# A hybrid convolution and attention block: wider steps for taps and attention, softmax scaled on ScalarE, norm sums in other PSUM banks

## The chip, the cores and the metric

The kernel runs on one core of a Trainium2 chip. The metric is the device time of one execution in microseconds (us); the time before is the median of three runs. Engines: TensorE (PE) multiplies matrices, VectorE (DVE) and ScalarE (ACT) work elementwise on SBUF and PSUM, GpSimd (POOL) elementwise on SBUF, and SyncE's queue (SP) issues the transfers.

## What is computed

```python
h = rmsnorm(x, norm_g)                                   # x: 2048 x 1024, fp32
proj = h @ w_in                                          # 1024 x 7680
glu_in, conv_gate, q, k, v, attn_gate, merge_logits = split(proj)

a, b = split(glu_in)                                     # convolution branch
c = depthwise_conv(a * sigmoid(b), w_dw, 31 taps, causal) + b_dw
c = silu(layernorm(c, ln_g, ln_b))                       # over the 1024 channels
y_conv = (c * silu(conv_gate)) @ w_conv_out

q, k = rope(q), rope(k)                                  # 16 q heads, 4 kv heads, 64 wide
s = (q @ k.T) * 64 ** -0.5                               # 128-wide sliding window
m = max(rowmax(s), sink);  p = exp(s - m)
a = (p / (sum(p) + exp(sink - m))) @ v
y_attn = (a * silu(attn_gate)) @ w_attn_out

g_conv, g_attn = split(sigmoid(merge_logits))
x = x + (g_conv * y_conv + g_attn * y_attn) @ w_out
return rmsnorm(x, final_norm_g)
```

## The kernel before

The 2048 positions are worked in two sweeps of 1024. Activations stand transposed (channels on partitions) as pairs of fp32r tiles, a rounded part and its remainder, and so do weights; each product takes three matmuls (rounded by rounded, rounded by remainder, remainder by rounded). A projection of 128 output channels over a sweep is one *item* (`project`): two halves of 512 positions, 24 matmuls each into one of three PSUM banks (`mm_ps`), and then an evacuation of the half by ACT or DVE. An item's weights are loaded and split one item ahead (`load_w`: SP loads, ACT casts, POOL subtracts).

A sweep runs 12 items for k, v and q with RoPE (`rope_items`, L426: DVE multiplies out of PSUM, POOL adds, ACT and DVE split, SP stores to DRAM), then 32 gate items (`gate_item`, L404: ACT applies Silu or Sigmoid into a `t2k` tile, which is stored to DRAM), then eight items `ya` (attention output), eight `yc` (convolution output) and sixteen blocks `o` (output projection). In between, ahead of items 0, 4, 8 to 28 of these 44 (`GLU_AFTER`), stand eight pairs of GLU items, one for each 128 channels of the convolution.

Only PE's order is written by hand; the other engines' orders are the framework's scheduling of the same program. The hand order comes from a planner with a clock of its own, the class `Line` (L160). It counts 0.2275 us for a matmul (`MM_US`), and `spend` puts in, after each three matmuls, what is due:

- *Taps.* The 31 taps of a channel tile (`conv_ops`, L359; DVE, L368) go to a queue `bg` when the tile's GLU is done. One leaves it every `line.every` us, `CONV_EVERY` at first.
- *Attention.* `start_attention` (L588) sets 32 steps of one kv head and 128 positions each, the n-th at 8.0 + n * `ATT_EVERY`. A step (`attention`, L512) comes in three parts, `LAT[0]` and `LAT[1]` apart: eight score matmuls `sc` (L526), masking and softmax (L533 to L548); four transposes `tpp` (L553) with a split (L555, L230) and selects for the two key blocks (L562, L564); four products `ov` (L573) with the sum (L577) and a store (`d_att`, L578). A step loads q and k for the next one (`load_qk`, L495).
- *Layer norm.* When the eighth tile has its last tap, `ln_chain` (L636) splits the channel sum into four `t2k` tiles, and after `LN_LAT[0]` sums over partitions by matmuls with ones (`ln_stats`, L606, in the bank of the scores, `sc_ps`); ACT copies the mean (L641). Eight `ln_center` follow, one every `LN_EVERY`; then `ln_chain2` does the same for the variance after `LN_LAT[1]`, with ACT's square root (L652), four reciprocals (`ln_recip`) and eight `ln_apply` (DVE product, ACT Silu, L634).
- *The attention output's inputs.* During the last gate item sixteen `aT` steps (`a_op`, L700) are put into the queue, 14 when the last attention is done, two when the norm is done. Before the first `ya` matmul, `line.finish()` empties the queue.

`slot` names one of 40 fixed SBUF places; `next_of` goes round in a ring of them. There are five `t2k` tiles for all uses.

Of the kernel before, what the change touches and what calls it, by code (L numbers as in the profile page):

```python
# [12 lines left out]
F32 = mybir.dt.float32  # L13
F32R = mybir.dt.float32r
I32 = mybir.dt.int32
AF = mybir.ActivationFunctionType
ALU = mybir.AluOpType
AX = mybir.AxisListType

P = 128  # L20
S = 2048
D = 1024
KC = D // P
T = 1024
NSWEEP = S // T
NB = T // P
TH = 512
# [5 lines left out]
GQ = NH // NKV  # L33
# [5 lines left out]
EPS = 1e-5  # L39
NEG = -1e30  # L40
MM_US = 0.2275
LN_LAT = (9.0, 15.0)
LN_EVERY = 2.4
GLU_AFTER = (0, 4, 8, 12, 16, 20, 24, 28)
CONV_EVERY = 2.0
ATT_EVERY = 13.4
LAT = (16.0, 12.0)
SCALE = HD ** -0.5


# [1 line left out]
def hybrid_block(ctx: ExitStack, tc: tile.TileContext, x, par_d, w_in, w_conv, sinks, w_attn, w_out,  # L52
                 fin_g, rope_t, out):
    nc = tc.nc
    pe, act, dve, pool = nc.tensor, nc.scalar, nc.vector, nc.gpsimd
# [4 lines left out]
    work = ctx.enter_context(tc.tile_pool(name="work", bufs=2))  # L60
    mm_ps = ctx.enter_context(tc.tile_pool(name="mm_ps", bufs=3, space=bass.MemoryType.PSUM))
    tp_ps = ctx.enter_context(tc.tile_pool(name="tp_ps", bufs=3, space=bass.MemoryType.PSUM))
    sc_ps = ctx.enter_context(tc.tile_pool(name="sc_ps", bufs=1, space=bass.MemoryType.PSUM))
# [5 lines left out]
    def f(ap):  # L69
        return ap.bitcast(F32)  # L70
# [7 lines left out]
    def slot(tag, shape, dt, name):  # L78
        n = int(np.prod(shape[1:]))
        full = HALO + T + 2 if tag in WIDE else 1024  # L80
        t = slots.tile([P, full], dt, tag=tag, name=name)
        v = t[:, 0:n]
        if len(shape) == 3:
            v = v.rearrange("p (a b) -> p a b", b=shape[2])
        elif len(shape) == 4:
            v = v.rearrange("p (a b c) -> p a b c", b=shape[2], c=shape[3])
        return v
# [6 lines left out]
    def next_of(key, tags):  # L94
        rot.setdefault(key, cycle(range(len(tags))))
        return tags[next(rot[key])]
# [20 lines left out]
    ones = const.tile([P, P], F32R, name="ones")  # L117
# [9 lines left out]
    eps = eps[:, 0:1]  # L127
# [219 lines left out]
    def sweep(s):  # L347
# [147 lines left out]
        def load_qk(n):  # L495
            if n >= NKV * NB:
                return
            g, b = divmod(n, NB)
            blk = s * NB + b
            t = slot(next_of("qk", AT[11:14]), [P, 2, 4 * P], F32R, f"qk{s}_{n}")  # L500
            q, k = t[:, 0, :].rearrange("p (r t) -> p r t", t=P), t[:, 1, :].rearrange("p (a t) -> p a t", a=2)
            qk[n] = (q, k)
            fs = slice(g * HH, (g + 1) * HH)
            for i in range(4):
                nc.sync.dma_start(out=f(q[i * HH:(i + 1) * HH]), in_=d_q[i // 2, i % 2, fs, blk, :, :])
            k0 = max(blk - 1, 0) * P
            nk = (blk + 1) * P - k0
            for i in range(4):
                nc.sync.dma_start(out=f(k[i * HH:(i + 1) * HH, :, 2 * P - nk:]),
                                  in_=d_k[:, i % 2, fs, k0:k0 + nk].rearrange("a p t -> p a t"))  # L510

        def attention(n):  # L512
# [7 lines left out]
            for h in range(GQ):  # L520
                for j in range(2):
# [2 lines left out]
                    else:  # L524
                        o, r = sc[:, h], k[:, j]
                    pe.matmul(out=o, lhsT=q[:, h, :], rhs=r, start=(j == 0), stop=(j == 1))  # L526
            ss = slot(next_of("ss", AT[4:7]), [P, 1024], F32, f"ss{u}")
            sb = ss[:, 0:512].rearrange("p (h q) -> p h q", q=P)
            oT = ss[:, 512:768].rearrange("p (a q) -> p a q", q=P)
            if first:  # L530
# [1 line left out]
            else:  # L532
                act.copy(sb, sc[:, :, 0, :])  # L533
            dve.copy_predicated(out=sb, mask=causal_i, data=sc[:, :, 1, :])
            st = work.tile([P, 6, GQ], F32, tag="st", name=f"st{u}", bufs=3)
            mx, ngm, es, den, rinv, dlt = (st[:, i, :] for i in range(6))
            hd = slice(g * GQ, (g + 1) * GQ)
            dve.tensor_reduce(out=mx, in_=sb, axis=AX.X, op=ALU.max, negate=True)
# [6 lines left out]
                               bias=ngm[:, h:h + 1], accum_out=den[:, h:h + 1])  # L545
            dve.tensor_tensor(out=den, in0=den, in1=es, op=ALU.add)
            dve.reciprocal(out=rinv, in_=den)  # L547
            pool.tensor_tensor(out=sb, in0=sb, in1=rinv.unsqueeze(2).broadcast_to([P, GQ, P]), op=ALU.mult)  # L548
            yield 0.96, LAT[0]

            tpp = tp_ps.tile([P, GQ, P], F32, tag="tp", name=f"tpp{u}")
# [5 lines left out]
            if first:  # L557
                seq = [(v_of(g, b), pt)]
            else:
                pc = slot(next_of("pc", AT[9:11]), [P, 2, GQ, P], F32R, f"pc{u}")  # L560
                for i in range(2):
                    pool.affine_select(out=pc[:, i], in_=f(pt[:, i]), pattern=[[0, GQ], [1, P]],  # L562
                                       compare_op=ALU.is_ge, fill=0.0, base=0, channel_multiplier=-1)
                    pool.affine_select(out=pt[:, i], in_=f(pt[:, i]), pattern=[[0, GQ], [-1, P]],  # L564
                                       compare_op=ALU.is_gt, fill=0.0, base=0, channel_multiplier=1)
                seq = [(v_of(g, b), pc), (v_of(g, b - 1), pt)]
            yield 0.44, LAT[1]

# [19 lines left out]
        def start_attention():  # L588
            load_qk(0)
            for n in range(NKV * NB):  # L590
                line.after(8.0 + n * ATT_EVERY, attention(n))


        ln = {}
# [10 lines left out]

        def ln_stats(parts, name):  # L606

            st = sc_ps.tile([P, T], F32, tag="sc", name=f"{name}{s}")
            for half in range(2):
                for i in range(2):  # L610
                    pe.matmul(out=st[:, half * TH:(half + 1) * TH], lhsT=ones, rhs=parts[half][i],
                              start=(i == 0), stop=(i == 1))
            return st

        def ln_center(c):
# [20 lines left out]
        def ln_chain():  # L636
            parts = ln_parts(csum, "csum")
            yield 0.0, LN_LAT[0]
            st = ln_stats(parts, "lnmu")
            ln["mu"] = slot(AT[15], [P, T], F32, f"mu{s}")  # L640
            act.copy(ln["mu"], st)  # L641
            line.every = LN_EVERY
            line.bg.extend([lambda c=c: ln_center(c) for c in range(KC)])
            line.bg.append(lambda: line.start(ln_chain2()))
            yield 4 * MM_US, 0.0

        def ln_chain2():
            parts = ln_parts(ln["v"], "vsum")
            yield 0.0, LN_LAT[1]
            st = ln_stats(parts, "lnvar")  # L650
            ln["r"] = slot(AT[14], [P, T], F32, f"rstd{s}")
            act.activation(out=ln["r"], in_=st, func=AF.Sqrt, bias=eps)  # L652
            work_ops = [lambda i=i: ln_recip(i) for i in range(4)]
            work_ops += [lambda c=c: ln_apply(c) for c in range(KC)]
            work_ops.append(lambda: ln.update(done=True))
            line.bg.extendleft(reversed(work_ops))
            yield 4 * MM_US, 0.0
# [3 lines left out]
        gates += [gate_item("ma", C_MA, AF.Sigmoid, e) for e in range(KC)]  # L661
        gates += [gate_item("mc", C_MC, AF.Sigmoid, e) for e in range(KC)]
        line.every = CONV_EVERY
        others = rope_items("k", E_K, store_k) + [v_item(i) for i in range(2)]
        for r in range(GQ):
            others += rope_items(f"q{r}_", E_Q + 2 * r, store_q(r))
# [4 lines left out]
        if s == 0:  # L671
# [8 lines left out]
                    yield ((lambda: None) if half == i == 0 else item[half][0],) + item[half][1:]  # L680
            glu_after.pop(0)
        for i, item in enumerate(others):
            if glu_after and i == glu_after[0]:
                glu_after.pop(0)
                items = glu_items(KC - 1 - len(glu_after))
                yield from items
            if s or i:
                yield item
            if i == nqkv:
                start_attention()  # L690


        aT, uT = [[None] * KC, [None] * KC], []
# [200 lines left out]
```

## Time and profile before

| | |
|---|---|
| median of 3 runs | 2235.6 us (2234.0 to 2236.23) |
| the profiled execution | 2237.25 us |
| its span, first to last instruction | 2235.5 us |
| busy: PE, DVE, POOL, ACT | 94%, 67%, 45%, 41% |
| PE's mean granted clock | 0.968 |
| first PE instruction; last | 8.5 us; 2229 us |

A page of the profile gives busy time by engine, the chain of waits that ended last, and groups of instructions by line: operation, output and inputs, count, busy time in us, mean ns of one, then the idle time of the engine just before them and what ended it. The view of waits has rows "engine, tile and line, waited for whom: us in total, times, longest". A timeline row has start (us), duration (us), engine, line, operation; in square brackets the idle time ahead of it and what ended that. A window row gives the window, its length, and each engine's busy time (with its count of instructions), then PE's granted clock, the share of the DMA engines, GB/s. The first row of matmuls of each stage gives the stage boundaries used below.

### The profile page before, as it was taken

The page shows a single profiled execution, that of the slowest core. Times are in us where ns is not written, and L with a number is a line of the kernel's source. Part 1 is how long each engine was busy: PE and PEld are TensorE (multiplying, and loading weights), DVE is VectorE, ACT ScalarE, POOL GpSimd, SP SyncE. Part 2 cuts the span into 40 slices and gives each one's busy share as a digit, 9 for nine tenths or more (in the row PEclk, how much of TensorE's full clock was granted, in tenths as well). Part 3 has the DMA queues.
Part 4 walks back from the last instruction along what each step waited for, and adds up shares of the span by engine and source line. Part 5 has one row for each costly group of instructions (what it writes and reads, how often), then busy time and mean ns, then how long its engine had stood idle before and what let it go on. Part 6 is the DMA issues. An engine that isn't in the chain of part 4 may idle for free. (4 is left out here: it accounts for less than half of the span.)

```text
span 2235.5 us, 26989 instructions
## 1 busy us (share of the span) xinstructions
PE 2105.8 (94%) x9256; PEld 1694.8 (76%) x9256; DVE 1505.9 (67%) x1804; ACT 918.0 (41%) x1925; POOL 995.9 (45%) x738
## 2 busy tenths in 40 slices
PE   7999899899999889999999999999899899899998
PEld 6877678778777766888887777777777777668887
DVE  4999988697797417123678999696797973261224
ACT  5212254555557723123522113545556486231212
POOL 4446556575655421241033545665656654112400
PEclk9999999999999997999999999999999999889999
DMA  5223433323333247334322324333333333572331
GB/s 182 80 90 108 134 98 96 106 93 114 102 110 110 90 146 240 104 100 168 114 95 90 108 90 123 111 105 108 101 97 104 100 106 104 172 222 92 99 127 76
DMA packets 186873, 257.81 MB, mean 115 GB/s; under 512 B 21616, under 2 KB 87280, under 8 KB 186736
## 3 DMA queue, kind: packets, MB, share of 16 engines
q1 hardware_dynamic: 186736, 256.09, 36.1%
q8 instruction: 73, 1.20, 0.2%
q14 instruction: 64, 0.52, 0.1%
HBM read 184.70 MB, written 71.30 MB: 115 GB/s over the span
## 5 line engine op out<-in xcount | busy, mean ns | idle before, releaser
L368 DVE SCALAR_TENSOR_TENSOR cv<-glu,par,cv 128x1024 f32<-128x1024 f32 x480 | 764.9, 1594 | 9.5
L259 PE MATMUL mm_ya<-aT,whi_ya 128*128 128x512 f32 x512 | 183.9, 435 | 22.6 <-ACT aT L271 18.7
L564 POOL TENSOR_SCALAR_AFFINE_SELECT pt<-pt 128x512 fp32r<-128x512 f32 x120 | 128.0, 1069 | 126.0 <-DVE st L541 53.4
L815 PE MATMUL o<-wo,mT 128*128 128x512 f32 x768 | 180.7, 394 | 0.0
L259 PE MATMUL mm_ga<-hT,whi_ga 128*128 128x512 f32 x512 | 163.7, 401 | 13.8 <-DVE rb_q__1_10475 L438 3.4
L815 PEld LDWEIGHTS o<-wo,mT 128*128 128x128 f32 x768 | 143.3, 188 | 31.4
L259 PE MATMUL mm_gb<-hT,whi_gb 128*128 128x512 f32 x512 | 166.1, 406 | 0.0
L259 PE MATMUL mm_cg<-hT,whi_cg 128*128 128x512 f32 x512 | 163.2, 400 | 0.0
L259 PE MATMUL mm_ag<-hT,whi_ag 128*128 128x512 f32 x512 | 162.1, 398 | 0.0
L259 PE MATMUL mm_ma<-hT,whi_ma 128*128 128x512 f32 x512 | 161.7, 397 | 0.0
L259 PE MATMUL mm_mc<-hT,whi_mc 128*128 128x512 f32 x512 | 161.5, 397 | 0.0
L562 POOL TENSOR_SCALAR_AFFINE_SELECT pc<-pt 128x512 fp32r<-128x512 f32 x120 | 123.3, 1030 | 84.6 <-ACT pt L555 76.2
L259 PE MATMUL mm_yc<-uT,whi_yc 128*128 128x512 f32 x512 | 159.4, 392 | 0.0
L259 PEld LDWEIGHTS mm_ya<-aT,whi_ya 128*128 128x128 f32 x512 | 103.1, 201 | 70.0 <-ACT aT L271 35.5
L548 POOL TENSOR_TENSOR ss<-ss,st 128x512 f32<-128x512 f32 x64 | 94.8, 1482 | 127.4 <-DVE st L547 34.9
L544 ACT ACTIVATE ss<-ss,st 128x128 f32<-128x128 f32 x256 | 99.8, 391 | 119.1 <-DVE st L539 118.8
L230 POOL TENSOR_TENSOR wlo_ya<-raw_ya,whi_ya 128x512 fp32r<-128x512 f32 x32 | 42.6, 1330 | 190.3 <-ACT whi_ya L240 190.3
L259 PEld LDWEIGHTS mm_ga<-hT,whi_ga 128*128 128x128 f32 x512 | 96.7, 192 | 36.6 <-issue 15.4
L259 PEld LDWEIGHTS mm_gb<-hT,whi_gb 128*128 128x128 f32 x512 | 98.8, 196 | 21.4
L259 PEld LDWEIGHTS mm_mc<-hT,whi_mc 128*128 128x128 f32 x512 | 97.3, 191 | 21.7
L259 PEld LDWEIGHTS mm_yc<-uT,whi_yc 128*128 128x128 f32 x512 | 96.1, 188 | 21.9
L259 PEld LDWEIGHTS mm_cg<-hT,whi_cg 128*128 128x128 f32 x512 | 96.6, 193 | 20.5
(357 smaller groups left out, 4741.2 us busy)
## 6 DMA issues: line engine op xcount, KB each, us to landing
qk<-d_q SPq DMA_DIRECT2D x256, 64.0 KB, 2.7
qk<-d_k SPq DMA_DIRECT2D x240, 64.0 KB, 2.3
raw_gb<-in_w_in_dram SPq DMA_DIRECT2D x34, 256.0 KB, 2.7
raw_ga<-in_w_in_dram SPq DMA_DIRECT2D x34, 256.0 KB, 3.1
raw_ag<-in_w_in_dram SPq DMA_DIRECT2D x32, 256.0 KB, 3.0
d_ag<-ag SPq DMA_DIRECT2D x32, 256.0 KB, 2.5
d_att<-ss SPq DMA_DIRECT2D x64, 128.0 KB, 1.8
raw_cg<-in_w_in_dram SPq DMA_DIRECT2D x32, 256.0 KB, 2.8
```

What stands on the lines that cost most here:

```text
L230: eng.tensor_tensor(out=out_, in0=full, in1=f(hi), op=ALU.subtract)
L259: pe.matmul(out=ps, lhsT=a, rhs=b, start=(k == 0 and i == 0), stop=(k == KC - 1 and i == 2))
L368: dve.scalar_tensor_tensor(out=cv[c], in0=glu[c][:, j:j + T], scalar=tap(c, j), in1=cv[c], op0=ALU.mult, op1=ALU.add)
L544: act.activation(out=sb[:, h, :], in_=sb[:, h, :], func=AF.Exp, scale=SCALE, bias=ngm[:, h:h + 1], accum_out=den[:, h:h + 1])
L548: pool.tensor_tensor(out=sb, in0=sb, in1=rinv.unsqueeze(2).broadcast_to([P, GQ, P]), op=ALU.mult)
L562: pool.affine_select(out=pc[:, i], in_=f(pt[:, i]), pattern=[[0, GQ], [1, P]], compare_op=ALU.is_ge, fill=0.0, base=0, channel_multiplier=-1)
L564: pool.affine_select(out=pt[:, i], in_=f(pt[:, i]), pattern=[[0, GQ], [-1, P]], compare_op=ALU.is_gt, fill=0.0, base=0, channel_multiplier=1)
L815: pe.matmul(out=ps, lhsT=a[:, c0:c0 + P], rhs=r, start=(k == 0 and i == 0), stop=(k == KC - 1 and i == 2))
```

## The change

Six edits, all in how the same work is placed:

1. Taps leave the queue every 2.4 us of the planner's clock instead of 2.0.
2. Attention steps are 14.5 apart instead of 13.4; the latencies inside a step are 22 and 14 instead of 16 and 12. The ring of softmax tiles `ss` has four places instead of three (it takes one from the ring `qk`, three to two), and the small statistics tile `st` has four buffers instead of three.
3. Attention is set up before the first item after the last q item (a GLU pair's first) instead of after that pair, and its first step is due 22 us from there instead of 8.
4. The division of the softmax is four ACT copies with a scale for each partition, one for each head, instead of one POOL product with a broadcast.
5. The four POOL selects become two, each over both parts of the split.
6. The norm's sums go to two tiles of the projections' banks (`mm_ps`) instead of the scores' bank, with the copy and the square root in two halves; the latencies before them are 14 and 30 instead of 9 and 15.

```diff
-LN_LAT = (9.0, 15.0)
+LN_LAT = (14.0, 30.0)
-CONV_EVERY = 2.0
-ATT_EVERY = 13.4
-LAT = (16.0, 12.0)
+CONV_EVERY = 2.4
+ATT_EVERY = 14.5
+LAT = (22.0, 14.0)
...
-            t = slot(next_of("qk", AT[11:14]), [P, 2, 4 * P], F32R, f"qk{s}_{n}")
+            t = slot(next_of("qk", AT[11:13]), [P, 2, 4 * P], F32R, f"qk{s}_{n}")
...
-            ss = slot(next_of("ss", AT[4:7]), [P, 1024], F32, f"ss{u}")
+            ss = slot(next_of("ss", AT[4:7] + AT[13:14]), [P, 1024], F32, f"ss{u}")
...
-            st = work.tile([P, 6, GQ], F32, tag="st", name=f"st{u}", bufs=3)
+            st = work.tile([P, 6, GQ], F32, tag="st", name=f"st{u}", bufs=4)
...
-            pool.tensor_tensor(out=sb, in0=sb, in1=rinv.unsqueeze(2).broadcast_to([P, GQ, P]), op=ALU.mult)
+            for h in range(GQ):
+                act.activation(out=sb[:, h, :], in_=sb[:, h, :], func=AF.Copy, scale=rinv[:, h:h + 1])
...
-                for i in range(2):
-                    pool.affine_select(out=pc[:, i], in_=f(pt[:, i]), pattern=[[0, GQ], [1, P]],
-                                       compare_op=ALU.is_ge, fill=0.0, base=0, channel_multiplier=-1)
-                    pool.affine_select(out=pt[:, i], in_=f(pt[:, i]), pattern=[[0, GQ], [-1, P]],
-                                       compare_op=ALU.is_gt, fill=0.0, base=0, channel_multiplier=1)
+                pool.affine_select(out=pc, in_=f(pt), pattern=[[0, 2], [0, GQ], [1, P]],
+                                   compare_op=ALU.is_ge, fill=0.0, base=0, channel_multiplier=-1)
+                pool.affine_select(out=pt, in_=f(pt), pattern=[[0, 2], [0, GQ], [-1, P]],
+                                   compare_op=ALU.is_gt, fill=0.0, base=0, channel_multiplier=1)
...
-                line.after(8.0 + n * ATT_EVERY, attention(n))
+                line.after(22.0 + n * ATT_EVERY, attention(n))
...
-            st = sc_ps.tile([P, T], F32, tag="sc", name=f"{name}{s}")
+            st = []
             for half in range(2):
+                st.append(mm_ps.tile([P, TH], F32, tag="mm", name=f"{name}{s}_{half}"))
                 for i in range(2):
-                    pe.matmul(out=st[:, half * TH:(half + 1) * TH], lhsT=ones, rhs=parts[half][i],
-                              start=(i == 0), stop=(i == 1))
+                    pe.matmul(out=st[half], lhsT=ones, rhs=parts[half][i], start=(i == 0), stop=(i == 1))
             return st
...
-            act.copy(ln["mu"], st)
+            for half in range(2):
+                act.copy(ln["mu"][:, half * TH:(half + 1) * TH], st[half])
...
-            act.activation(out=ln["r"], in_=st, func=AF.Sqrt, bias=eps)
+            for half in range(2):
+                act.activation(out=ln["r"][:, half * TH:(half + 1) * TH], in_=st[half], func=AF.Sqrt, bias=eps)
...
         for i, item in enumerate(others):
+            todo = [item] if s or i else []
             if glu_after and i == glu_after[0]:
                 glu_after.pop(0)
-                items = glu_items(KC - 1 - len(glu_after))
-                yield from items
-            if s or i:
-                yield item
+                todo = glu_items(KC - 1 - len(glu_after)) + todo
             if i == nqkv:
-                start_attention()
+                todo[0] = ahead(todo[0], start_attention)
+            yield from todo
```

`ahead(item, work)` is an item that does `work` when its first matmul is planned.

More of the change, by code (lines that the diff above doesn't have):

```diff
@@ L663, in sweep, with ahead, blocks @@
         line.every = CONV_EVERY
+        def ahead(item, work):
+            def blocks():
+                work()
+                yield from item[1]()
+            return item[0], blocks
         others = rope_items("k", E_K, store_k) + [v_item(i) for i in range(2)]
```

## The prediction

> **What bounds the kernel now.** I read the page first, then sums by stage, then who TensorE (PE) waits for, then single waits in the timeline.
>
> ```profile
> span 2235.5 us, 26989 instructions
> ...
> PE 2105.8 (94%) x9256; PEld 1694.8 (76%) x9256; DVE 1505.9 (67%) x1804; ACT 918.0 (41%) x1925; POOL 995.9 (45%) x738
> ```
>
> PE is busy for 94% and every other engine far less. So the time is PE's work plus what PE loses, and a change that leaves the matmuls alone can only move the loss. The view by windows says in which stage it lies. I cut it at the first matmul of a stage: for each sweep projections with RoPE, then gates with attention, then the attention output `ya`.
>
> ```profile
> 17.80:259.80 242.00, 230.06 (x1012) 185.58 (x1011) 214.95 (x186) 58.77 (x109) 116.48 (x74) 0.99 0.33 101
> 259.80:827.50 567.70, 534.25 (x2434) 435.50 (x2433) 409.60 (x496) 318.30 (x670) 314.96 (x241) 0.97 0.34 106
> 827.50:943.10 115.60, 104.32 (x386) 75.97 (x385) 53.80 (x75) 28.26 (x48) 22.80 (x17) 0.87 0.57 181
> ...
> 1126.10:1365.60 239.50, 227.84 (x985) 184.21 (x984) 213.05 (x191) 48.18 (x96) 104.75 (x67) 0.99 0.32 99
> 1365.60:1935.00 569.40, 537.04 (x2442) 438.17 (x2442) 411.75 (x496) 316.95 (x670) 330.92 (x249) 0.97 0.34 106
> 1935.00:2051.80 116.80, 105.51 (x386) 76.69 (x385) 53.10 (x75) 28.26 (x48) 21.80 (x17) 0.84 0.57 179
> ```
>
> Columns after the length: busy PE, PE's weight loads, DVE, ACT, POOL, then the granted clock. The undisturbed price of an item (48 matmuls) comes from the chain of waits, where the eight `yc` items run without a gap; that of one attention step on PE from the timeline.
>
> ```profile
> 2051.93 88.57 PE mm_yc L259 x384
> ```
> ```profile
> 702.20 1.12 PE L526 MATMUL sc<-qk 128*128 128x256 f32 x8
> 703.15 0.63 PE L259 MATMUL mm_ma<-hT,whi_ma 128*128 128x512 f32 x2
> ...
> 705.24 0.62 PE L573 MATMUL ov<-pc,vt 128*128 128x512 f32 x2
> ...
> 706.51 0.70 PE L259 MATMUL mm_ma<-hT,whi_ma 128*128 128x512 f32 x2
> ```
>
> An item is 88.57 / 8 = 11.07 us. An attention is 0.95 us of scores (702.20 to 703.15) and 1.27 us of products and transposes (705.24 to 706.51), 2.22 us. So what each stage loses against full speed, idle time and half-clock matmuls together:
> - RoPE stage, 20 items, 221.4 us, and 5.3 and 1.8 us of transposes at the planner's prices (12 and 4 times 0.44): losses 15.3 and 16.3, together 31.6 us.
> - Gate stage, 40 items (442.8) and 32 attentions (71.0), 1.8 for the norm's sums: 515.6; losses 52.1 and 53.8, together 105.9 us.
> - `ya`, 8 items, 88.6: losses 27.0 and 28.2, together 55.2 us.
>
> All other stretches run at full speed. Who PE waits for:
>
> ```profile
> PE tpp L553 <- POOL ss L548: 52.5, 30, 4.9
> PE mm_ya L259 <- ACT aT L271: 18.7, 14, 3.7
> ...
> PE sc L526 <- ACT rstd L652: 5.1, 2, 3.8
> ...
> PE sc L526 <- ACT mu L641: 3.5, 2, 2.3
> ...
> PE mm_ga L259 <- DVE rb_q__1_10475 L438: 3.4, 1, 3.4
> ```
>
> In the gate stage it is the transpose of the probabilities, which waits for POOL's normalisation. PE's idle time there in sweep 0 is 567.70 - 534.25 = 33.5 of the 52.1 us lost: each microsecond of stall costs 1.56 us, the rest being slow matmuls behind it (granted clock 0.97, and 0.84 in the second `ya`). But POOL is only the last link:
>
> ```profile
> 1659.08 1.12 PE L526 MATMUL sc<-qk 128*128 128x256 f32 x8
> ...
> 1661.20 7.70 DVE L368 SCALAR_TENSOR_TENSOR cv<-glu,par,cv 128x1024 f32<-128x1024 f32 x4
> ...
> 1668.93 0.73 DVE L534 COPY_PREDICATED ss<-causal,sc 128x512 f32<-128x512 int32 x1
> 1672.72 0.40 ACT L544 ACTIVATE ss<-ss,st 128x128 f32<-128x128 f32 x1 [3.63 <-DVE st L539]
> 1674.28 0.39 ACT L544 ACTIVATE ss<-ss,st 128x128 f32<-128x128 f32 x1
> 1677.45 0.18 DVE L547 RECIPROCAL st<-st 128x4 f32<-128x4 f32 x1
> 1679.92 2.02 POOL L548 TENSOR_TENSOR ss<-ss,st 128x512 f32<-128x512 f32 x1
> 1681.99 0.66 PE L553 MATMUL tpp<-ident_r,ss 128*128 128x128 f32 x4 [0.91 <-POOL ss L548]
> ```
>
> Scores end at 1660.03 and the transpose can start at 1681.99, 22.0 us later, where the planner allowed 16. Nine of these 22 us are VectorE (DVE): four convolution taps, 7.70 us, stand ahead of the masking copy. POOL's own part is 4.4 us (1677.63 to 1681.94 with its wait). DVE is therefore what is late, in the RoPE stage too:
>
> ```profile
> 100.00:260.00 160.00, 149.28 (x638) 120.34 (x637) 153.16 (x125) 28.78 (x52) 77.83 (x48) 0.99 0.33 98
> ```
> ```profile
> 100.00:260.00 160.00, 109.47 (x67) 0.99 0.33 98
> ```
>
> DVE is busy for 153.2 of 160 us there, 109.5 of it 67 taps (1.63 us each).
>
> **The change, part by part.** Planner times are worked out with the code's own clock: 10.92 us an item, 2.31 an attention, and an item is really 1.014 times that.
>
> *Taps every 2.4 instead of 2.0.* A channel tile's 31 taps take 74.4 instead of 62 planner us, while a tile comes every 65.5 (six items) before attention begins and about 76 with it. So taps no longer come in bursts with pauses, but evenly, and fall behind by 9 us a tile. Until the last q item ends, about 12 taps fewer are issued: 12 x 1.63 = 20 us less for DVE, where PE loses 15.3 to 16.3 us a sweep. Its longest wait there is 3.4 us; taking 20 us out of the queue covers it. I keep a quarter for local bursts: 31.6 falls to 7. Bounds: 0 and 20.
>
> *Wider attention steps (14.5), more latency (22, 14).* From scores to transpose the planner now allows 22 where the attention above took 22.0 with POOL and with four taps ahead of it. What DVE has to do beside taps, from a window of most of sweep 0's attention (all engines, then the taps' line alone):
>
> ```profile
> 280.00:620.00 340.00, 318.33 (x1468) 260.89 (x1467) 271.76 (x330) 187.15 (x424) 202.62 (x157) 0.96 0.34 102
> ```
> ```profile
> 280.00:620.00 340.00, 180.36 (x117) 0.96 0.34 102
> ```
>
> The window holds 25 steps of 13.6 us (13.4 x 1.014), so 91.4 / 25 = 3.7 us a step is not taps: 25% of the new 14.7 us. Taps, 1.54 us here, take 76% of DVE at one in 2.03 us and 63% at one in 2.43: with 27% beside them 103% within a burst before, 88% now. The queue stops growing. POOL's 4.4 us become four ACT copies. The chain should take 22.0 - 4.4 + 1.2 = 18.8, and with one or two taps (1.93) fewer ahead 15 to 17 us: the 52.5 us of waits go. What is late next is then no longer in this chain but in the norm's (below). The ring of `ss` tiles grows to four, which follows the longer life (37.4 us over 14.5); `qk` shrinks to two, and nothing waits, since a load is still issued one step ahead and its tile's last reader ran a step before.
>
> *Attention begun at the last q tile.* It starts two items (21.8) earlier, but with 22 instead of 8 us: the first scores come 7.8 us earlier, the last 31 x 1.1 - 7.8 = 26.3 later, and their product 34.3 later. From the last q item to the `aT` steps there are 41 items, 32 attentions and the norm's sums (1.8), 523 planner us; the last product stands at 22 + 31 x 14.5 + 37.4 = 509. The first loads of q and k now stand on SP's queue ahead of a gate's weights and wait for the last RoPE stores: one stall of up to 2 us a sweep.
>
> *Normalising by copies.* I have no row of this operation. The nearest are ACT's exponential and its copy of the same size:
>
> ```profile
> L368 DVE SCALAR_TENSOR_TENSOR cv<-glu,par,cv 128x1024 f32<-128x1024 f32 x480 | 764.9, 1594 | 9.5
> ...
> L548 POOL TENSOR_TENSOR ss<-ss,st 128x512 f32<-128x512 f32 x64 | 94.8, 1482 | 127.4 <-DVE st L547 34.9 <-ACT ss L576 33.4 <-ACT pt L555 30.0
> L544 ACT ACTIVATE ss<-ss,st 128x128 f32<-128x128 f32 x256 | 99.8, 391 | 119.1 <-DVE st L539 118.8
> ```
> ```profile
> L309 ACT CAST hT<-hs 128x128 fp32r<-128x128 f32 x64 | 14.5, 295 | 18.2 <-DVE hs L304 18.2
> ```
>
> Four are 1.2 to 1.6 us; I take 1.2 (a copy with no accumulator): 75 us more for ACT over the kernel, off PE's path, and 94.8 less for POOL. But ACT now stops in order for DVE's reciprocal, with projection evacuations and weight casts behind it (the rival below). The merged selects do the same elements in two instructions for four; their product has 14 us for it. Zero. [...] In the rows, the four taps above took 1.93 us each against 1.59 on average, POOL's product 2.02 against 1.48: while both run, both are slower. Its absence can give DVE up to 1.5 us a step back; the sum takes none.
>
> *Norm sums in projection banks.* The 8.6 us of `sc` waits (5.1 + 3.5) are in the 105.9. In their place two of three projection banks are taken in mid-item, so the next half-item may wait for ACT to empty a bank: from 0 to the 3.4 us that a projection waits for a bank above, twice a sweep; I take 2 us a time, 4 us a sweep. The old waits are gone either way, so the cost cannot be below nothing.
>
> *LN_LAT 14 and 30.* Four of the five `t2k` tiles are held from the split to the sums, for 14 + 30 instead of 9 + 15 planner us. Gate evacuations then share one tile and a store:
>
> ```profile
> 722.52 6.13 SPq L408 DMA_DIRECT2D d_ma<-ma  x2
> ...
> 726.41 1.28 ACT L407 ACT_TABLE_LOAD   x1 [2.38 <-DMA d_ma<-ma]
> ```
>
> ACT stood 2.4 us for such a store. With projections' evacuations behind it and PE behind those, 0 to 7 us a sweep (three such waits of 2.4); I take 2. Walking the code's queue, the last tap moves from 393 to 422 planner us after the last q item; the norm behind it takes 14 + 19 (eight centrings) + 30 + 29 (twelve steps) and 2 of sums: it ends near 516, some 7 ahead of the `aT` steps and 49 later than before.
>
> *Sum.* Gate stage: 1 (first load) + 4 + 2 + 1 (late last steps) = 8 us idle a sweep, times 1.56 = 13, so 105.9 falls to 26. `ya` stays at 55.2: its tiles are gated at the same point, between DMA loads. Gain 24.6 + 79.9 = 104.5. The profiled execution took 2237.25 (span 2235.5), giving 2132.7; the median of the runs is 1.65 lower: **2131**.
>
> **Rivals.**
> [...]
> 2. *The norm ends too late:* its 7 us of margin go in an ACT full of table loads, and the `aT` steps queue behind it. At 8 to 16 us late a sweep, times 1.56: 25 to 50 us in all, 2156 to 2181. For it: the last steps of the norm, of attention and of the gates now fall together. Against: DVE has caught up by then.
> 3. *ACT becomes the bound, slower than before.* In the window 280 to 620 above ACT waits for DVE:
>
> ```profile
> ACT ss L544 <- DVE st L539: 38.2, 15, 6.6
> ACT ss L576 <- DVE ss L577: 21.5, 5, 7.0
> ...
> ACT st L542 <- DVE st L541: 12.8, 10, 7.1
> ```
>
> In 25 steps ACT is busy 187.15 / 25 = 7.5 us a step and stands 72.5 / 25 = 2.9 for DVE. To that come 1.2 of copies, 0.2 of longer step, and the wait for the reciprocal, 3.0 us in the attention above (1674.67 to 1677.63). Sum 14.8, against a step of 14.7. It decides from there: if DVE's queue adds one tap (1.93 us) to that, all 64 steps stretch by 2.0 us: 2131 + 128 = 2259. Against it: the waits are those of a DVE with taps in bursts. [...] In the rows above DVE is the fuller engine.
> 4. *No effect on the waits:* DVE is still full, transposes still wait, only the RoPE stage gains: 2236 - 25 = 2211.
>
> **How the numbers follow.** Forecast 0.61, rivals 1 to 4: 0.15, 0.14, 0.06, 0.04. The range goes from 2108 (rival 1 with all bounds at their lower end, some 5 us less) to 2180 (nearly all of rival 2), leaving out a tenth. A measurement tells 0.2% (4.5 us) from no change. Faster: 0.61 + 0.15 + 0.14 + 0.04, less a little for a mixed outcome, 0.93; slower 0.05; same 0.02.
>
> **What would show it.** Right: `tpp` no longer waits for anything for over 5 us in all; `sc` waits vanish and projection tiles wait for ACT by about 8 us; RoPE stages near 230, gate stages near 529, `ya` still 115. Wrong: `tpp` waits for ACT copies by tens of us, ACT busy or waiting for DVE through every step (rival 3); or `ya` over 125 with the norm's Silu ahead of `aT` (rival 2).

## The result, and the profile after

The changed kernel takes 2160.86 us (median of 4 runs, 2159.24 to 2163.33) against 2235.91 for the kernel before (a fourth run added to the three above): a ratio of 0.9667, 95% interval 0.965 to 0.9684. The profiled execution took 2162.24 us, 75.0 less than the 2237.25 of before, where 104.5 less was forecast. Of the kernels below, one run of e3_pool_norm took 3446 us at a granted clock of 0.568; its median and ratio are those of its three other runs.

First the head of the page of after, which answers to that of before:

```profile
span 2160.5 us, 27022 instructions
...
PE 2081.9 (96%) x9256; PEld 1683.8 (78%) x9256; DVE 1474.0 (68%) x1804; ACT 1005.3 (47%) x2195; POOL 819.8 (38%) x554
```

PE has the same 9256 matmuls and is busy for 24 us less, at a mean granted clock of 0.976 instead of 0.968. ACT is busy for 87 us more, POOL for 176 less. The windows of after, cut at the same first matmuls as those of before (window, length, busy PE, weight loads, DVE, ACT, POOL, granted clock, DMA share, GB/s):

```profile
18.30:263.90 245.60, 233.94 (x1011) 188.62 (x1010) 215.49 (x187) 59.02 (x110) 118.38 (x75) 0.97 0.33 100
263.90:789.90 526.00, 520.14 (x2433) 428.88 (x2432) 387.14 (x493) 358.78 (x801) 228.01 (x152) 0.99 0.37 113
789.90:907.20 117.30, 102.57 (x385) 76.13 (x385) 55.14 (x76) 29.21 (x49) 22.18 (x17) 0.87 0.56 179
...
1090.30:1332.50 242.20, 230.49 (x986) 186.25 (x985) 214.18 (x192) 48.19 (x97) 106.56 (x68) 0.97 0.32 98
1332.50:1862.80 530.30, 523.63 (x2441) 429.44 (x2440) 398.51 (x494) 362.17 (x807) 238.01 (x152) 1.00 0.37 113
1862.80:1976.80 114.00, 103.59 (x386) 75.15 (x385) 54.34 (x76) 28.54 (x49) 22.39 (x17) 0.87 0.59 184
```

Taking the prediction's full-speed price off each stage (226.7 and 223.2 for RoPE, 515.6 for the gates, 88.6 for `ya`), both sweeps together lose:

| stage | before | forecast | after |
|---|---|---|---|
| RoPE | 31.6 | 7 | 37.9 |
| gates and attention | 105.9 | 26 | 25.1 |
| `ya` | 55.2 | 55.2 | 54.1 |

The gate stage gave 80.8 us, nearly what was forecast. The RoPE stage, from which 24.6 were to come, lost 6.3. That is the whole miss. Who PE waits for now:

```profile
PE mm_ya L259 <- ACT aT L271: 19.5, 13, 4.0
...
PE ov L573 <- POOL pc L562: 4.0, 3, 3.4
PE mm_ga L259 <- DVE rb_q__1_10509 L438: 3.5, 1, 3.5
...
PE mm_ga L259 <- DVE rb_q__1_1294 L438: 3.4, 1, 3.4
PE ov L573 <- POOL pt L564: 3.4, 5, 1.3
...
PE mm_q_b L259 <- DVE ra_q__0_10394 L432: 2.4, 1, 2.4
PE mm_mc L259 <- ACT mc L407: 2.4, 1, 2.4
```

The 52.5 us of `tpp` and the waits of `sc` are gone. The waits of the RoPE stage (`rb_q`, `ra_q`) and of `ya` stand as they were. The timeline shows why `tpp` no longer waits. This is the twentieth step of the second sweep, whose counterpart of before the prediction quotes:

```profile
1614.81 1.12 PE L526 MATMUL sc<-qk 128*128 128x256 f32 x8
...
1624.16 0.59 ACT L533 COPY ss<-sc 128x512 f32<-128x512 f32 x1
...
1626.61 0.73 DVE L534 COPY_PREDICATED ss<-causal,sc 128x512 f32<-128x512 int32 x1
...
1633.96 0.18 DVE L547 RECIPROCAL st<-st 128x4 f32<-128x4 f32 x1
...
1635.53 1.27 ACT L549 ACTIVATE ss<-ss,st 128x128 f32<-128x128 f32 x4
...
1641.73 0.49 PE L554 MATMUL tpp<-ident_r,ss 128*128 128x128 f32 x3
```

The chain is no quicker here (it is the longest of after): the mask copy starts 11 us after the scores end, the copies end at 1636.8, 21 us after the scores. But the transposes come only at 1641.7. Over all 64 steps, the chain from the last score matmul to the last normalising instruction took 15.6 us on average before (longest 23.7) and 14.8 after (20.9); from the scores to the first transpose PE left 19.1 us before and 23.1 after. Before, 33 of the 64 chains were longer than 16.2 us, the shortest distance from scores to transposes in that trace; in after that distance is 22.1, and no chain is longer. The longer delay covers the longest chain.

The groups that changed form, from the groups by line and shape:

```profile
L562 POOL TENSOR_SCALAR_AFFINE_SELECT pc<-pt 128x1024 fp32r<-128x1024 f32 x60 | 90.8, 1513 | 195.1 <-DVE pt L230 190.2 <-DVE st L546 4.9
...
L549 ACT ACTIVATE ss<-ss,st 128x128 f32<-128x128 f32 x256 | 81.8, 391 | 28.3 <-DVE st L547 28.2
```

A copy shows 391 ns, as long as the exponential and not the 295 assumed; but four in a row take 1.27 to 1.28 us in the timeline, since each starts 0.29 us after the one ahead (median), before that one has ended.

### The profile page after: what moved, and what is told of

Same layout as the page of the kernel before. It is cut to its first block, busy times and chain, and to the rows that moved or that the text cites. A ratio compares the mean times of both kernels' runs of the same rounds, so it can differ in the third digit from the quotient of the medians.

```text
span 2160.5 us, 27022 instructions
## 1 busy us (share of the span) xinstructions
PE 2081.9 (96%) x9256; PEld 1683.8 (78%) x9256; DVE 1474.0 (68%) x1804; ACT 1005.3 (47%) x2195; POOL 819.8 (38%) x554
## 4 chain that ended last, share of the span: by engine, by line
PE 52%; DVE 31%; ACT 6%; DMA 4%; issue 4%; POOL 3%; SPq 0%; DVEq 0%; ACTq 0%; POOLq 0%
DVE cv L368 21%; PE o L823 8%; PE mm_yc L259 8%; PE mm_ya L259 7%; PE mm_ga L259 6%; PE mm_mc L259 6%; PE mm_ma L259 6%; PE mm_ag L259 5%; PE mm_gb L259 3%; DMA latt<-d_att 2%; PE ov L573 1%; PE sc L526 1%; DVE ss L534 1%; ACT ss L544 1%; DVE st L538 1%
## 5 line engine op out<-in xcount | busy, mean ns | idle before, releaser
L368 DVE SCALAR_TENSOR_TENSOR cv<-glu,par,cv 128x1024 f32<-128x1024 f32 x480 | 735.5, 1532 | 7.6
L259 PE MATMUL mm_ya<-aT,whi_ya 128*128 128x512 f32 x512 | 180.9, 429 | 25.1 <-ACT aT L271 19.5
L259 PE MATMUL mm_ga<-hT,whi_ga 128*128 128x512 f32 x512 | 169.2, 413 | 14.3 <-DVE rb_q__1_10509 L438 3.5
L562 POOL TENSOR_SCALAR_AFFINE_SELECT pc<-pt 128x1024 fp32r<-128x1024 f32 x60 | 90.8, 1513 | 195.1 <-DVE pt L230 190.2
L230 POOL TENSOR_TENSOR wlo_gb<-raw_gb,whi_gb 128x512 fp32r<-128x512 f32 x34 | 60.1, 1780 | 145.7 <-ACT whi_gb L240 140.5
L259 PEld LDWEIGHTS mm_mc<-hT,whi_mc 128*128 128x128 f32 x512 | 95.0, 188 | 23.7 <-ACT mc L407 3.4
L259 PEld LDWEIGHTS mm_gb<-hT,whi_gb 128*128 128x128 f32 x512 | 96.7, 191 | 20.9
L259 PEld LDWEIGHTS mm_ag<-hT,whi_ag 128*128 128x128 f32 x512 | 94.4, 188 | 19.7
L259 PEld LDWEIGHTS mm_ma<-hT,whi_ma 128*128 128x128 f32 x512 | 94.3, 188 | 19.6
```

The source lines that it names most:

```text
L230: eng.tensor_tensor(out=out_, in0=full, in1=f(hi), op=ALU.subtract)
L259: pe.matmul(out=ps, lhsT=a, rhs=b, start=(k == 0 and i == 0), stop=(k == KC - 1 and i == 2))
L368: dve.scalar_tensor_tensor(out=cv[c], in0=glu[c][:, j:j + T], scalar=tap(c, j), in1=cv[c], op0=ALU.mult, op1=ALU.add)
L562: pool.affine_select(out=pc, in_=f(pt), pattern=[[0, 2], [0, GQ], [1, P]], compare_op=ALU.is_ge, fill=0.0, base=0, channel_multiplier=-1)
```

## The experiments

After the result, the theory was this: only PE's order is the planner's, the other engines' is the framework's; so the delay that the planner grants between PE's steps is what took the waits away, and a wider interval of taps can't empty DVE's queue in the RoPE stage. The rival: the interval took the load off DVE in the gate stage, and something new, the tile `rb` or the copies, holds the RoPE stage and the rest back. The expectations were written as the runs went. Where they use letters, A is that theory; B is the other view that each one states, C says that the RoPE stage's waits come from the taps at hand, D that `ya` hangs on when its inputs are planned, E that it hangs on DVE's remainders.

All kernels are timed against the kernel before on the same chip, so two of them are compared by their ratios; 0.001 is 2.2 us. Stage lengths are those of the profiled execution.

| kernel | median us | ratio, 95% interval | RoPE | gates | `ya` |
|---|---|---|---|---|---|
| after | 2160.86 | 0.9667 (0.965 to 0.9684) | 245.6, 242.2 | 526.0, 530.3 | 117.3, 114.0 |
| e1_taps_2us | 2181.51 | 0.9766 (0.9751 to 0.9781) | 243.6, 239.6 | 537.8, 539.5 | 115.4, 116.1 |
| e2_steps_only | 2175.35 | 0.974 (0.9723 to 0.9757) | 243.6, 239.5 | 531.5, 541.8 | 115.3, 116.8 |
| e5_third_pair_later | 2172.82 | 0.9725 (0.971 to 0.974) | 214.3, 212.4 | 559.8, 569.9 | 115.1, 115.4 |
| e4_second_rb | 2160.67 | 0.9675 (0.9658 to 0.9692) | 243.6, 240.3 | 525.6, 530.4 | 114.9, 116.5 |
| e3_pool_norm | 2153.0 | 0.9634 (0.9614 to 0.9654) | 242.0, 242.2 | 522.6, 528.5 | 115.8, 115.1 |
| e13_dve_norm | 2170.48 | 0.9712 (0.9696 to 0.9728) | 245.6, 238.7 | 527.9, 542.3 | 113.3, 116.2 |
| e9_four_selects | 2161.61 | 0.967 (0.9652 to 0.9688) | 244.5, 242.3 | 525.5, 529.7 | 117.4, 116.6 |
| e6_norm_back | 2167.46 | 0.9708 (0.9691 to 0.9725) | 245.4, 241.3 | 529.8, 532.9 | 117.3, 114.8 |
| e8_start_back | 2165.27 | 0.9696 (0.9679 to 0.9712) | 243.6, 242.2 | 533.1, 528.5 | 116.4, 115.7 |
| e7_tail_early | 2157.19 | 0.966 (0.9645 to 0.9674) | 243.6, 240.3 | 525.9, 531.5 | 115.0, 113.4 |
| e10_aT_pool | 2169.21 | 0.9705 (0.9689 to 0.9722) | 243.6, 239.5 | 526.2, 533.1 | 120.8, 118.9 |
| e11_pool_norm_tail | 2150.24 | 0.9612 (0.9594 to 0.9629) | 243.7, 241.3 | 520.4, 528.3 | 116.3, 113.5 |

**The interval of the taps.** After, with the old interval:

```diff
-CONV_EVERY = 2.4
+CONV_EVERY = 2.0
```

> The changed kernel with the tap interval back at 2.0. Theory A (the interval only ranks instructions; VectorE's order is a list schedule that fills VectorE with whatever tap is ready): within 6 us of 2161, RoPE stages still 242 to 246 us with the same four waits of 3.4 us. Theory B (the prediction's: the interval sets VectorE's load): RoPE stages equal too, since they did not move when the interval was widened, but the gate stages get their bursts back and lose 10 us or more each: 2180 or above.

The time is the one of theory B. The RoPE stage is not longer (243.6 and 239.6), so the interval buys nothing there. The gate stages are 11.8 and 9.2 us longer: there it is worth 21 of the 80.8, which theory A did not expect. But it is not B's way either. The windows of the taps' line alone say that it is not a matter of how many taps are issued; first those of after, then those of this run (DVE's busy time and number of taps):

```profile
100.00:260.00 160.00, 108.24 (x66) 0.96 0.33 97
284.00:624.00 340.00, 193.25 (x133) 0.99 0.36 109
```
```profile
100.00:260.00 160.00, 109.45 (x67) 0.97 0.33 98
282.00:622.00 340.00, 193.68 (x133) 0.99 0.36 109
```

With a fifth more planner time between taps, as many are done: 66 and 67 in the RoPE stage, 133 and 133 in the gates. In the traces of before and after DVE's instructions stand in the same order up to 262 us, all 207 of them. Only PE's order is written by hand. This fits an interval that for DVE only ranks the taps among the other work that the framework schedules; where DVE is full nothing changes.

What PE waits for in this run says where the 21 us lie:

```profile
PE ov L573 <- POOL pt L564: 7.4, 10, 1.5
PE lnmu L612 <- ACT ma L407: 5.6, 2, 5.4
PE ov L573 <- POOL pc L562: 4.3, 3, 3.4
...
PE mm_mc L259 <- ACT ma L407: 3.7, 1, 3.7
...
PE mm_mc L259 <- ACT whi_mc L240: 3.0, 1, 3.0
```

At the norm's sums and at `mm_mc` PE waits 12.3 us for ACT, against 4.0 in after (`mm_mc` 2.4, `lnvar` 1.6); at `ov` it waits 11.7 for POOL, against 7.4. The interval moves the norm, too: the planner starts it with the last tap, and the mean's sums stand at 655.6 and 1735.8 us in this run, at 690.7 and 1754.6 in after, though the last taps are done at nearly the same time (635.7 for 638.3 us in the first sweep). So more than half of the 14.8 us that PE is idle beyond after's 12.5 in these stages stands at the norm's sums and at `mm_mc`, for an ACT that is busy with a softmax or with the norm's own work there. How much of the 21 us is the norm's place and how much the order of the taps was not tried apart.

**The attention steps alone.** The kernel before with the step, the latencies and the rings of after:

```diff
-ATT_EVERY = 13.4
-LAT = (16.0, 12.0)
+ATT_EVERY = 14.5
+LAT = (22.0, 14.0)
```

> The kernel before with only the attention steps widened (14.5 apart, latencies 22 and 14) and the rings that go with it; POOL still normalises, taps, norm and start as before. Theory A (the latency allowed between scores and transposes is what takes the waits away): most of the gain, 2160 to 2175, the transposes' waits for POOL under 6 us in all. Rival (taking the product off POOL shortens the chain and is what counts): less than half of the gain, 2200 or above, over 20 us of waits left.

This is most of the gain: 0.026 of the 0.0333 (the median is just over the upper end of theory A's range). The gate stages lose 42.1 us (531.5 + 541.8 - 1031.2) where before lost 105.9. `tpp` no longer waits; what is left is this, in the waits of the run:

```profile
PE ov L573 <- POOL pc L562: 8.2, 4, 4.4
PE sc L526 <- ACT rstd L652: 5.1, 2, 4.0
PE ov L573 <- POOL pt L564: 3.9, 4, 1.5
```

The step and the latencies were not tried apart, but the chains of this run decide between them. With POOL's product still in them they take 14.5 us on average, and 24 of the 64 still take longer than the 16.2 us of before, up to 23.4. A wider step alone would have left these late; PE waits for none of them, because the transposes come 23.6 us after the scores on average, never sooner than 22.1.

**The RoPE stage.** After with the third GLU pair, one of those ahead of items of the RoPE stage, moved behind it:

```diff
-GLU_AFTER = (0, 4, 8, 12, 16, 20, 24, 28)
+GLU_AFTER = (0, 4, 12, 15, 18, 21, 25, 28)
```

> The changed kernel with the GLU pairs ahead of items 0, 4, 12, 15, 18, 21, 25, 28 instead of every fourth, so that the third channel tile's taps do not exist while the last two q pairs run. Theory C (the RoPE stage's waits come from the number of taps that VectorE has at hand, whatever their planned interval): the waits of the last two q pairs go (2.3 and 3.4 us a sweep, 18 us in all with the slow matmuls behind them), while the gate stages may lose some to denser taps: 2140 to 2155, and RoPE stages shorter by 8 to 10 us apart from the 22 us of the moved pair. Rival (VectorE and POOL pass the RoPE products to and fro, taps or not): the waits stay, 2158 or above.

```profile
18.50:232.80 214.30, 208.37 (x915) 168.54 (x914) 160.58 (x154) 56.01 (x103) 102.84 (x71) 0.98 0.35 110
232.80:792.60 559.80, 543.07 (x2530) 445.45 (x2528) 430.46 (x525) 362.58 (x808) 249.76 (x157) 0.99 0.35 109
```

With the pair's own 22.1 us added back, the RoPE stages take 236.4 and 234.5, 9.2 and 7.7 less than in after, and DVE is busy for 75% instead of 88% of them. PE's idle time there falls from 11.7 us in each sweep to 5.9 and 7.9, and of the 33 DVE instructions that are gone from the first stage 30 are taps. So what PE loses there does come from taps in DVE's way, but from taps that exist, not from those that the planner has let go. The gate stages, less the pair, are 11.7 and 17.5 longer, and `ov` waits 18.5 us for POOL. The gain is more than given back.

A second place for the tile `rb` changed nothing (0.9675). Two of the four `rb_q` waits fell from 3.4 to 1.9 us, but the same two did so in e7_tail_early below, which has one place:

```diff
-                b = slot(AT[6], [P, 2, TH], F32, f"rb{s}_{name}_{half}")
+                b = slot((AT[6], AT[13])[half], [P, 2, TH], F32, f"rb{s}_{name}_{half}")
```

> The changed kernel with a second place for the RoPE product tile rb (one for each half), so that the second half's products need not wait for POOL's reading of the first half's. Theory A1 (the RoPE stage's waits come from this one tile's chain between VectorE and POOL): the four waits of 3.4 us go, with the slow matmuls behind them some 20 us: 2135 to 2147. Theory B (VectorE is simply full of taps there): the waits stay or move, within 6 us of 2161.

**Who normalises.** After with POOL's product again, and after with the same product on DVE:

```diff
-            for h in range(GQ):
-                act.activation(out=sb[:, h, :], in_=sb[:, h, :], func=AF.Copy, scale=rinv[:, h:h + 1])
+            pool.tensor_tensor(out=sb, in0=sb, in1=rinv.unsqueeze(2).broadcast_to([P, GQ, P]), op=ALU.mult)
```

> The changed kernel with the softmax normalised by the one POOL product again. Theory A: the chain from scores to transposes grows by 1 to 2 us, still under the 23 us allowed: 2157 to 2170. Rival (the copies count): the transposes wait for POOL again, 2180 or above.

> The kernel after, with the normalising done by one VectorE product behind the reciprocal, instead of four ScalarE copies. By the theory that the copies cost time because ScalarE works its queue in order, and the weight casts, evacuations and the rounding of pt stand behind copies that wait for VectorE's reciprocal, any other engine does: some 2153 to 2157 us, as with the product on GpSimd, pt rounded earlier, GpSimd's wait for whi_ag and whi_ma back from 61 and 53 us to some 15. The product needs 0.68 to 0.75 us by the mask copy and the row maximum of the same size, 45 us more for VectorE over the kernel, and nothing waits for VectorE in between. By the rival that VectorE is the engine that is late, those 45 us stand ahead of the masks and taps of the next steps: 2165 to 2175, with ov waits over 10 us. If the copies never cost anything and the 7 us were scatter: 2158 to 2163.

POOL's product has the lowest ratio of the three and DVE's the highest: 0.9634, 0.9667, 0.9712. With POOL's the chain did not grow, as theory A had it, but took 14.2 us on average for 14.8, and the time lies below both expectations. From the groups of the run with DVE's product:

```profile
L368 DVE SCALAR_TENSOR_TENSOR cv<-glu,par,cv 128x1024 f32<-128x1024 f32 x480 | 739.4, 1540 | 7.4
L548 DVE TENSOR_TENSOR ss<-ss,st 128x512 f32<-128x512 f32 x64 | 63.9, 999 | 1.1
```

It takes 1.0 us a step, not 0.7, on the engine that is late; time and `ov` waits (7.9 and 3.6 us for POOL's selects) are those of the rival. Between POOL and ACT the intervals just touch (0.9654 and 0.965); the last run below repeats the comparison and there they are apart. Where the copies cost: the cast of `pt` (ACT, behind the transposes) ends 6.25 us after the transposes on average with copies, 4.83 with POOL's product. With copies ACT stands 28.2 us for DVE's reciprocal in all (the row of L549 above), a wait that POOL's product does not put on it. That fits, but the run with DVE's product has 5.77 without any copy (a fuller DVE may keep ACT waiting elsewhere; that was not shown); so the copies' share of it is not isolated. POOL's waits for ACT's weight casts, on which the second of these expectations leaned, don't tell the theories apart: they stayed at 60 to 71 us with DVE's product.

**The selects, the norm and the start.** Each was put back alone, in after:

```diff
-                pool.affine_select(out=pc, in_=f(pt), pattern=[[0, 2], [0, GQ], [1, P]],
+                for i in range(2):
+                    pool.affine_select(out=pc[:, i], in_=f(pt[:, i]), pattern=[[0, GQ], [1, P]],
...
```

> The changed kernel with the four POOL selects of 512 elements again in place of two of 1024. In the changed kernel's trace a select of 1024 takes 1.5 us where one of 512 took 1.05, so merging saves 1.1 us of POOL a step. Theory A (the products' 14 us hold it either way): within 6 us of 2161. Rival (the selects' chain is what the products wait for): the waits of ov for POOL grow from 7.4 to over 15 us, 2170 or above.

No difference beyond the noise, and `ov` waits 7.3 us for POOL as in after (7.4).

```diff
-LN_LAT = (14.0, 30.0)
+LN_LAT = (9.0, 15.0)
...
-                st.append(mm_ps.tile([P, TH], F32, tag="mm", name=f"{name}{s}_{half}"))
+            st = sc_ps.tile([P, T], F32, tag="sc", name=f"{name}{s}")
...
```

> The changed kernel with the norm's sums in the scores' bank again and the latencies 9 and 15. Theory A: the waits of the scores for the mean and the square root come back, 8.6 us with 5 us of slow matmuls: 2170 to 2178. Rival (the shorter hold on the t2k tiles is worth as much): within 6 us of 2161.

0.9708 against 0.9667, with intervals apart: the norm's edits are worth some 9 us, a little under theory A's 2170 to 2178. Of the old waits one of `sc` for the square root (3.2 us) came back, and one of `lnvar` for the scores' bank (3.5 us); the two of `mm_mc` and `lnvar` for ACT (4.0) went. Banks and latencies were put back together, so which of them counts is open.

```diff
-                line.after(22.0 + n * ATT_EVERY, attention(n))
+                line.after(8.0 + n * ATT_EVERY, attention(n))
...
-                todo[0] = ahead(todo[0], start_attention)
-            yield from todo
+            yield from todo
+            if i == nqkv:
+                start_attention()
```

> The changed kernel with attention set up after the GLU pair again and the first step due 8 us later: everything of attention 7.8 planner us later. Theory A: no wait hangs on it, within 6 us of 2161. Rival (the last product then falls behind the point where the aT steps are planned): ya longer by 4 us or more a sweep, 2168 or above.

0.9696 against 0.9667, some 6 us slower, but the intervals overlap by 0.0005, so a cost is not shown. The first gate stage is 7 us longer, the second is not, and `ya` did not lengthen as the rival had it; `ov` waits 13.3 us for POOL instead of 7.4.

**What bounds `ya`.** It lost 54 to 55 us in both kernels. Two tries, in after: the `aT` steps put into the queue one item earlier, and their remainders made by POOL.

```diff
+            if i == len(others) - 2:
+                start_tail()
             yield from todo
...
-        start_tail()
         yield ya_item(0, True)
```

> The changed kernel with the aT steps released one gate item (11 us) sooner, as soon as attention and norm are planned as done. Theory D (the loss of the ya stage is set by the point at which the aT steps are planned, their loads taking 2.8 us each in a row): half of the ya loss goes, 10 us a sweep: 2138 to 2150, ya near 105. Rival (the queue of ACT, full of the norm's Silu, is what holds aT up): ya unchanged, within 6 us of 2161.

```diff
-            put_split(dst, g, dve)
+            put_split(dst, g, lo_eng)
```

> The changed kernel with the remainder of the aT tiles made by POOL instead of VectorE. Theory E (the ya stage starves because VectorE makes an aT in 2.0 us, product, wait for ACT's cast, remainder, one after the other): VectorE's part falls to 0.7 us a tile, ya falls by 5 us or more a sweep: 2140 to 2152. Rival (the loads bound it, with the DMA engines 73 to 77% busy and five t2k tiles): ya within 3 us of 114 to 117, 2156 or above.

Earlier planning took 2.3 and 0.6 us off `ya`, within what profiles differ by. POOL's remainders made it longer by 3.5 and 4.9, and the kernel slower than after (0.9705); PE then waits for POOL:

```profile
PE mm_ya L259 <- POOL aT L230: 17.5, 21, 1.7
PE mm_ya L259 <- ACT aT L271: 12.0, 9, 2.9
```

The remainder is on the path; the point at which the `aT` steps are planned is not what limits `ya`. Windows of after show where the loss is:

```profile
789.90:835.00 45.10, 30.37 (x69) 16.78 (x69) 28.35 (x40) 14.12 (x24) 5.05 (x4) 0.66 0.73 233
835.00:907.20 72.20, 72.20 (x318) 59.35 (x317) 26.79 (x37) 15.09 (x25) 17.13 (x13) 1.00 0.46 145
```

All of it lies in the first 45 us, in which the DMA engines are busy for 73%, DVE for 63%, and PE at 0.66 of its clock. Around it (785 to 835 us) SP's loads wait 18.5 us for DVE (11.3 for its remainders, 7.2 for its products), which points at the five `t2k` tiles and DVE's part of the chain. Whether they or the loads set the pace was not tried.

**The best of both.** After with POOL's product and the earlier `aT` steps:

> The changed kernel with the softmax normalised by POOL again and the aT steps released one item sooner. If the two gains add (7 and 4 us): 2146 to 2153, faster than both kernels. If they share one cause: 2153 to 2157.

It takes 2150.24 us: 0.9612, interval 0.9594 to 0.9629, clear of after's and faster than both kernels. That lies where adding gains would put it, but its interval overlaps that of POOL's product alone (0.9614 to 0.9654), and early `aT` steps alone were not clear of after, so that they gain anything is not shown. Against the early `aT` steps alone (0.966, interval 0.9645 to 0.9674), the only difference is who normalises, and the intervals are apart: the copies cost some 10 us here. A version with 18 instead of 14 ahead of the products has no time, so whether a longer delay there would take the 6.8 us that `ov` still waits is open.

## Why the prediction was right, and where not

The time fell inside the range, 30 us above the forecast, and the reasons behind it fare differently.

*Taps every 2.4: "about 12 taps fewer are issued ... I keep a quarter for local bursts: 31.6 falls to 7".* This step failed. (A quarter of 31.6 would also be 7.9, not 7.) It took the planner's clock for DVE's schedule. As many taps were issued (66 for 67), the waits stayed, and the term of -24.6 came out as +6.3. The 6.3 are not DVE's either: PE was idle for 11.7 us in each of the two stages, as before (11.9 and 11.7). The difference is the clock after the last wait, shown below (0.81 and 0.80 granted instead of 1.00; 3.0 and 2.9 us in the two sweeps), and other kernels with this stage unchanged took 242.0 to 245.6 and 238.7 to 242.3.

*Wider steps: "the 52.5 us of waits go".* Right, and the size too: 105.9 fell to 25.1, forecast 26. The chain was forecast at 15 to 17 us and took 14.8. (POOL's part of the quoted chain, 1677.63 to 1681.94, is 4.3 us, not 4.4; nothing hangs on it.) But the reason given, that DVE's queue stops growing, was only half of it: DVE was busy for 271.76 of 340 us before and is for 276.27 now, with 16 taps more in that window. The steps and latencies alone removed 63.8 of the 80.8, and the average chain had been 15.6 before, just under the delay: it was the longer half of the chains that waited, and the delay now covers all. The interval is worth 21 in after (shares taken one at a time need not add up), not by thinning the taps; more than half of the waiting that it saves stands at the norm's sums and `mm_mc`, and how far the order of the taps has a part in it is open.

*Copies: 1.2 us a step, "off PE's path".* The size was right (1.27), the place wrong: with POOL's product the kernel is 7 to 11 us faster. So the 104.5 held a cost priced at nothing. *Selects: zero.* Right.

*Idle time of the gate stage: 8 us a sweep (first load 1, norm's banks 4, `t2k` tiles 2, late steps 1).* It was 5.9 and 6.7, by other items: 7.4 of `ov` for POOL's selects, which had been left out, 2.4 of `mm_mc` for ACT, 1.6 of the norm's variance, in both sweeps together. The 2.4 are not the term for `t2k` tiles: in the 9 us before that evacuation ACT was busy for all but 1, with the norm's squares and a softmax. No score matmul waited at all, so the first loads of q and k cost nothing. A microsecond of it cost 1.8 and 2.2, not 1.56. The errors cancel: that 25.1 came so near to 26 is luck in this part.

*`ya` stays at 55.2.* 54.1, right. The last tap came earlier than before (637 and 1707 us against 668 and 1777), not 29 planner us later; the margin was never used.

*Rivals.* The first, that POOL's absence frees DVE, carries a chance of 0.15 and the lower end of the range, 2108; no run shows a gain of its own behind them. In the trace of before, taps beside POOL's work were slower: 1.28 us on average for the 174 with no POOL instruction beside them, 1.84 for the 173 with POOL busy for 90% of their time or more. Over all 480, taps took 1532 ns for 1594, but 1548 with POOL's product back (e3_pool_norm), and the kernel with that product is the faster one. The second (norm too late) and the third (ACT the bound) did not come: `ya` is unchanged, and ACT is busy for 358.78 of 526 us. The fourth, no effect on the waits, is false for `tpp` and true for the RoPE stage. Of the three ways to normalise, DVE's product is the shortest, 1.0 us against 1.27 for the copies, and yet the kernel with it is the slowest, 0.9712 against 0.9667. DVE is the fuller engine (busy for 68% in after, ACT for 47%), and what is put on it stands ahead of masks and taps; that this is the reason was the expectation, and the longer `ov` waits (11.5 us for 7.4) agree with it.

## What to carry to other kernels

Ask which engines obey the order that a planner writes down: where only TensorE's order is by hand, a spacing for other engines' work is a priority, and it doesn't thin their load. Where a wait comes from the longer ones of many chains and their average lies below the distance allowed, widen the distance before speeding up a link. Give a small step to the engine that is early at that point, here GpSimd (1.41 us a step, ratio 0.9634), and not to the one on which it is shortest, here VectorE (1.0 us, 0.9712).

## What the runs showed of the hardware

After a stall of the same length the granted clock was not always the same. At the end of the first RoPE stage PE stands for 3.4 us in both kernels. Windows of before and of after (the fields as in the stage windows above):

```profile
245.00:260.00 15.00, 11.56 (x50) 9.31 (x50) 14.69 (x12) 3.76 (x7) 6.74 (x4) 1.00 0.58 163
```
```profile
246.00:264.00 18.00, 14.58 (x52) 11.39 (x51) 15.81 (x13) 4.00 (x8) 9.38 (x6) 0.81 0.57 168
```

Before, the clock stayed at 1.00; after, it was 0.81. The 50 matmuls of the one window were busy for 11.56 us, the 52 of the other for 14.58. The second sweep shows the same pair (1.00 and 0.80), but e3_pool_norm, with the same interval, has the slow clock in its second RoPE stage alone (0.99 and 0.97 over the two stages): it differs from kernel to kernel. What decides it no run shows. A low clock was granted after a shorter stall, too: in this window of before PE stands for 2.1 of 3.5 us, at 1.00, and in the second one, half a microsecond later, it has 0.51:

```profile
301.00:304.50 3.50, 1.36 (x8) 0.86 (x7) 3.46 (x4) 2.76 (x6) 2.35 (x2) 1.00 0.20 75
305.00:308.50 3.50, 3.50 (x10) 2.73 (x9) 3.43 (x3) 0.47 (x1) 3.50 (x2) 0.51 0.23 76
```

A select on POOL over 128x1024 took 1513 ns in after, two over 128x512 took 1030 each before, and 910 each in the kernel after with four selects: merging saved a sixth to a quarter of POOL's time on them, and none of the kernel's. A remainder of 128x512 took DVE 0.70 us in after and POOL 1.41 in e10_aT_pool, which fits the longer `ya` where POOL made it.
